# Grouping the triangular inverses of a chunked RWKV-7 kernel by four head pairs instead of two

## The chip, the cores and the metric

The kernel runs on one core of a Trainium2 chip. Its engines are TensorE (PE, with its weight loads PEld), VectorE (DVE), ScalarE (ACT), GpSimd (POOL) and SyncE (SP), whose queue issues most of the transfers. The metric is the device time of one execution in microseconds; the median of three runs of the kernel before is 1001.98 us (1001.26 to 1002.05).

## The reference

One layer of a hybrid block, for 512 tokens and 16 meta tokens of 2048 features, in float32. One input projection gives the streams of an RWKV-7 branch (r, k, v, a gate, and low-rank paths for the decay and for a) and of a gated short convolution (B, C, h, a gate). Both branches go through one output projection, a residual sum and an RMS norm. The RWKV-7 branch is a recurrence per head over a 64 x 64 state:

```python
def step(S, inp):
    r_t, w_t, k_t, v_t, kk_t, b_t = inp
    sa = jnp.einsum('bhvk,bhk->bhv', S, kk_t)
    S = (S * w_t[:, :, None, :]
         - sa[..., None] * b_t[:, :, None, :]
         + v_t[..., None] * k_t[:, :, None, :])
    y_t = jnp.einsum('bhvk,bhk->bhv', S, r_t)
    return S, y_t
```

There are 16 heads of 64. The kernel does not step through the tokens: it cuts them into 9 chunks (the meta tokens, padded to 64, and 8 of 64) and solves each chunk at once. For that it needs, per head and chunk, the inverse of a 64 x 64 unit triangular matrix made of the products of the keys with each other.

## The kernel before

**The stream.** The input projection is 65 tiles of 128 output features. Each tile is 16 steps of the contraction, each of three matmuls (the weights and the input are split in a high and a low part in a fast float32 format, and high x high, high x low and low x high are summed), over one or two ranges of tokens. `mains` (line 501) yields one matmul at a time, in the order of `plan` (line 127): keys, receptances and values of two head pairs, their gates, and a convolution tile set (C, h, B, gc) after each two pairs. Weights come in halves of a tile (`prefetch`, line 162) into three buffers; ACT casts each quarter (line 158) and DVE or POOL subtracts (line 159), into six buffers.

**The order of PE.** PE's order is written by hand; the order of the other engines is made by a planner that works by costs and priorities (`ahead()` raises the priority). All small work of the RWKV branch is put between matmuls of the stream: `fill(ns)` (line 572) issues stream matmuls worth `ns`, at 0.43 ns a column, and what is called behind it comes next on PE. `until` issues stream until a tile is done. The amounts are in `FW` (line 42). `later(ns, fn)` (line 553) puts off a transfer until the stream has gone on by `ns`, behind the latest weight load on SP's queue.

**A head pair.** `prepare(i)` (line 648), for each of the 8 pairs of heads: low-rank products (`low_rank`, four fills of 2200), scaled keys `bk` and receptances `ar`, then the Gram products (line 703: 32 matmuls and 4 for the meta chunk) which DVE masks into `gt` (line 729). `gt` has two buffers, `gt0` and `gt1`, one for each pair of a set of two. Its parts go out to DRAM: the key blocks to a scratch `sg` (line 786), from which 16 x 16 diagonal blocks come back as `d`; other parts to `opd`, the operands of the recurrence. DVE inverts the 16 x 16 blocks (lines 811 to 831), and `y` goes to the scratch `sx` (line 846), from which it comes back as the block diagonal start of the inverse, `xT` and a shifted copy `xo` (`load_inverse`, line 835). `sx` has two buffers that are cleared once (lines 310 to 314).

**The inverse.** `invert(two)` (line 873) takes two pairs. After a long fill (`solve` 24500 and `more`), two levels double the size of the inverted blocks, from 16 to 32 and from 32 to 64. Each level is: a transpose of `xT` on DVE, a cluster T of 64 matmuls with `gt` as the stationary operand (line 895; line 935 at the second level, 32 x 32), copies out of PSUM on ACT (lines 902, 943), a cluster Z of 64 matmuls (lines 909 and 911; 950 and 954), and DVE's merging of the result into `xT` (line 919 to 926; 960). Between the four clusters stand the fills `tr`, `lev`, `cp` + `tr`, `lev`. The clusters' results lie in the two PSUM banks `tz`. At last `put_inverse` stores `xT` to `opd`.

The calls are, in order, `prepare(0)`, `prepare(1)`, `invert` of both, and so on for 2 and 3, 4 and 5, 6 and 7 (line 1104). After the last one a fill of 19500 (`begin`) leads to `recur` (line 982), which goes through the 9 chunks with fills of 2900, 2900 and 5200 in between; then `split_mix` (line 1126) builds the operands of the output projection with fills in between, the rest of the stream is issued, and the output projection follows (`product`, line 1278; DVE splits its weights at line 1256).

Of the kernel before, what the change touches and what calls it, by code (L numbers as in the profile page):

```python
# [9 lines left out]
F32 = mybir.dt.float32  # L10
# [8 lines left out]
P = 128  # L19
# [24 lines left out]
    evac=34, start=1062, lora=2200, gram=8000, meta={0: 2000}, gram_b=13500, gram2=5500, misc=2000, v=2000, vt=1000, solve=24500, more={0: 5500, 2: 2400},  # L44
    tr=3200, lev=3000, cp=4200, out=1500, begin=19500, p=2900, u=2900, s=5200, last=3700, mix=2600,
)
# [52 lines left out]
def hymba_kernel(ctx: ExitStack, tc: tile.TileContext, xt, xtok, front, w_in, w_out, pv, lup, cst, msk, gf, out):  # L99
# [89 lines left out]

    scr_x = [dp.tile([SCR], F32, tag=f"sx{b}", name=f"sx{b}", bufs=1) for b in range(2)]  # L190

# [5 lines left out]
    def tm(name):  # L197
        return tp.tile([P, LP], F32, tag="tm", name=name, bufs=3)
# [110 lines left out]
    nc.sync.dma_start(ms, msk)  # L309
    zt = tm("zt")  # L310
    nc.gpsimd.memset(zt, 0.0)
    for b in range(2):
        for o, n in ((0, 293), (293, 292)):
            nc.sync.dma_start(scr_x[b][P * o : P * (o + n)].rearrange("(p f) -> p f", p=P), zt[:, 0:n])
    nc.gpsimd.memset(smask, 1.0)
# [324 lines left out]
    def behind(dst, src):  # L640
        with tc.issue_after(state["dma"]):
            nc.sync.dma_start(dst, src)


    def stash_later(ns, *a):
        later(ns, lambda: stash(*a))

    def prepare(i):
        p = i % 2
        until("k", i)  # L650
# [160 lines left out]
        for m in (2, 4, 8):  # L811
            for b in range(16 // (2 * m)):
# [18 lines left out]
                nc.vector.tensor_reduce(out=sub(y, o, o + m, [[16, m], [1, m]]), in_=pq, op=ALU.add, axis=AX.X)  # L831
        xT = cq.tile([P, NCH, CH], F32, tag=f"xT{p}", name=f"xT{i}")
        xo = cq.tile([P, 4, CH], F32, tag=f"xo{p}", name=f"xo{i}")

        def load_inverse():
            for h in range(2):
                nc.sync.dma_start(xT[64 * h : 64 * h + 64], rows(sx, h))
                nc.sync.dma_start(
                    xo[64 - 64 * h : 128 - 64 * h],
                    bass.AP(  # L840
                        tensor=sx.tensor, offset=sx.offset + (8 + 4 * h) * BLK,
                        ap=[[CH, CH], [16 * BLK, 4], [1, CH]],
                    ),
                )
# [25 lines left out]
        fill(FW["vt"])  # L870
        return dict(gt=gt, xT=xT, xo=xo, i=i)

    def invert(two):
        first = two[0]["i"]
        both = range(2)
        fill(FW["solve"] + FW["more"].get(first, 0))
        run_pending(float("inf"))


        def wide(name):  # L880
            return tr(name)[:, 0 : 8 * CH].rearrange("p (q k s) -> p q k s", q=2, s=CH)

        xn = [tr(f"xn{t['i']}") for t in two]
        with ahead():
            for q in both:
                state["turned"] = nc.vector.transpose(
                    xn[q][:, CH:LP], two[q]["xT"][:, 1:NCH].rearrange("p c s -> p (c s)")
                ).ins
        fill(FW["tr"])
        z = [pz.tile([P, 2, 4, CH], F32, tag="tz", name=f"t{first}_{e}") for e in range(2)]  # L890
        for q in both:
            for k in range(4):
                for e, c in ((0, 2 * k + 2), (1, 2 * k + 1)):
                    for h, hs, ho in heads:
                        nc.tensor.matmul(
                            z[e][ho if e else hs, q, k], two[q]["gt"][hs, h, c, 0:CH],
                            xn[q][hs, c * CH : (c + 1) * CH], start=True, stop=True,
                        )
        ts_ = [wide(f"ts{first}_{e}") for e in range(2)]
        with ahead():  # L900
            for e in range(2):
                nc.scalar.copy(ts_[e], z[e])
        fill(FW["lev"])
        z = [pz.tile([P, 2, 4, CH], F32, tag="tz", name=f"z{first}_{e}") for e in range(2)]
        for q in both:
            xT, xo = two[q]["xT"], two[q]["xo"]
            for k in range(4):
                for h, hs, ho in heads:
                    nc.tensor.matmul(z[0][hs, q, k], ts_[0][hs, q, k], xT[hs, 2 * k + 2], start=True, stop=True)
                for h, hs, ho in heads:  # L910
                    nc.tensor.matmul(z[1][hs, q, k], ts_[1][ho, q, k], xo[ho, k], start=True, stop=True)
        quads = [(h, slice(64 * h, 64 * h + 32), slice(64 * h + 32, 64 * h + 64)) for h in range(2)]
        other = [slice(96, 128), slice(32, 64)]
        xn = [tr(f"xm{t['i']}") for t in two]
        with ahead():
            for q in both:
                xT, xo = two[q]["xT"], two[q]["xo"]
                for e in range(2):
                    nc.vector.copy_predicated(
                        xT[:, 2 - e : NCH : 2], ms.unsqueeze(1).to_broadcast([P, 4, CH]), z[e][:, q]  # L920
                    )
                nc.vector.transpose(xn[q][:, CH:LP], xT[:, 1:NCH].rearrange("p c s -> p (c s)"))
            for q in both:
                xT, xo = two[q]["xT"], two[q]["xo"]
                for h, lo, hi in quads:
                    nc.vector.tensor_copy(xo[other[h], :, 32:CH], xT[hi, 1 : NCH - 1 : 2, 32:CH])
        fill(FW["cp"])

        fill(FW["tr"])
        z = [pz.tile([P, 2, 4, 32], F32, tag="tz", name=f"t2{first}_{e}") for e in range(2)]  # L930
        for q in both:
            for k in range(4):
                for e, c in ((0, 2 * k + 2), (1, 2 * k + 1)):
                    for h, lo, hi in quads:
                        nc.tensor.matmul(
                            z[e][other[h] if e else hi, q, k], two[q]["gt"][lo, h, c, 32:CH],
                            xn[q][lo, c * CH : c * CH + 32], start=True, stop=True,
                        )
        ts_ = [wide(f"tm{first}_{e}") for e in range(2)]
        with ahead():  # L940
            for e in range(2):
                for h, lo, hi in quads:
                    nc.scalar.copy(ts_[e][hi, :, :, 0:32], z[e][hi])
        fill(FW["lev"])
        z = [pz.tile([P, 2, 4, 32], F32, tag="tz", name=f"z2{first}_{e}") for e in range(2)]
        for q in both:
            xT, xo = two[q]["xT"], two[q]["xo"]
            for k in range(4):
                for h, lo, hi in quads:
                    nc.tensor.matmul(  # L950
                        z[0][lo, q, k], ts_[0][hi, q, k, 0:32], xT[hi, 2 * k + 2, 32:CH], start=True, stop=True
                    )
                for h, lo, hi in quads:
                    nc.tensor.matmul(
                        z[1][lo, q, k], ts_[1][other[h], q, k, 0:32], xo[other[h], k, 32:CH], start=True, stop=True
                    )
        for q in both:
            for e in range(2):
                for h, lo, hi in quads:
                    nc.vector.tensor_copy(two[q]["xT"][lo, 2 - e : NCH : 2, 32:CH], z[e][lo, q])  # L960

        def put_inverse():
            for t in two:
                if t["i"] % 2 == 0:
                    stash(t["i"], t["xT"], O_X, CH)
                else:
                    for h, hs, ho in heads:
                        stash(t["i"], t["xT"][hs], O_X, CH, 64 - 64 * h, 64)

        later(5500, put_inverse)  # L970
        fill(FW["out"] if first < NPAIR - 2 else FW["begin"])

# [130 lines left out]

    for i in range(0, NPAIR, 2):
        invert([prepare(i), prepare(i + 1)])
    until("g", NPAIR - 1)
# [461 lines left out]
```

## Time and profile before

| | |
|---|---|
| median of three runs | 1001.98 us |
| profiled execution | 1002.49 us, of it 1000.7 us span |
| PE busy | 989.0 us (99%) |
| DVE busy | 684.7 us (68%) |
| ACT busy | 395.3 us (39%) |
| POOL busy | 271.2 us (27%) |
| transfers | 174.82 MB; under 512 bytes 121568 of 185036 packets |
| PE's granted clock | 0.997 of full speed |

PE's matmuls are pipelined and the ends in the profile are modelled, so what PE spends is read from the starts. In a row of a timeline stand the start in us from the span's start, the length, the engine, the line of the kernel, the operation, what is written and read, the shapes and how many instructions the row merges; in brackets the idle time of the engine before the row and what ended it. In a row of groups stand the count, the busy time and the mean length.

### The profile page before, as it was taken

The numbers are of one execution on the slowest core, as the hardware profiler recorded it, in microseconds if no ns is written. First come the engines' busy times: TensorE is split into PE (matmuls) and PEld (weight loads), VectorE is DVE, ScalarE is ACT, GpSimd is POOL, SyncE is SP. The second block draws the span as 40 slices with busy tenths as digits, with TensorE's granted clock in tenths as the row PEclk, the third lists the DMA queues.
The fourth block names the chain that finished last, engine by engine and source line by source line (L and its number), as shares of the span: only waits on it lengthen the run. The fifth ranks groups of instructions, "written<-read, shape, count | busy, mean of one in ns | idle before, by whom it ended". The sixth has DMA issues, their size and how long they took to land.

```text
span 1000.7 us, 23699 instructions
## 1 busy us (share of the span) xinstructions
PE 989.0 (99%) x9723; PEld 912.3 (91%) x9723; DVE 684.7 (68%) x1247; ACT 395.3 (39%) x729; POOL 271.2 (27%) x292
## 2 busy tenths in 40 slices
PE   9999999999999999999999999999999999999996
PEld 7999999999998999998999998889888898888885
DVE  6777965588765679744669644244554697997897
ACT  7553423344313434322434322222222426546463
POOL 0122424234233424232324222223332333001001
PEclk9999999999999999999999999999999999999998
DMA  9425586555575273854374746877773688697654
GB/s 327 149 84 147 145 208 158 152 149 140 154 178 165 93 196 99 200 147 119 86 196 110 195 135 195 293 220 236 213 219 97 175 261 213 185 319 176 158 126 168
DMA packets 185036, 174.82 MB, mean 175 GB/s; under 512 B 121568, under 2 KB 142816, under 8 KB 184416
## 3 DMA queue, kind: packets, MB, share of 16 engines
q1 hardware_dynamic: 182336, 164.40, 56.9%
q0 software_dynamic: 2304, 8.39, 4.8%
q8 instruction: 76, 1.25, 0.5%
q10 hardware_dynamic: 288, 0.52, 0.1%
q14 instruction: 32, 0.26, 0.1%
HBM read 136.92 MB, written 36.35 MB: 173 GB/s over the span
## 4 chain that ended last, share of the span: by engine, by line
PE 90%; DVE 5%; DMA 2%; issue 1%; SPq 0%; ACT 0%; POOL 0%; DVEq 0%; ACTq 0%; POOLq 0%
PE ps_v L346 9%; PE ps_k L346 9%; PE ps_h L346 9%; PE ps_g L346 9%; PE ps_r L346 9%; PE ps_B L346 9%; PE ps_gc L346 9%; PE ps_C L346 8%; PE M L1285 5%; PE P L1285 2%; DVE o L1256 2%; PE g L703 2%; PE Q L1285 1%; PE ps_lora L346 1%; PE zs L1048 1%
## 5 line engine op out<-in xcount | busy, mean ns | idle before, releaser
L158 ACT CAST w<-wr 128x512 fp32r<-128x512 f32 x252 | 153.4, 620 | 286.5 <-PE ps_C L346 48.2
L159 POOL TENSOR_TENSOR w<-wr,w 128x512 fp32r<-128x512 f32 x119 | 170.7, 1436 | 343.7 <-ACT w L158 290.9
L159 DVE TENSOR_TENSOR w<-wr,w 128x512 fp32r<-128x512 f32 x133 | 98.1, 743 | 114.4 <-ACT w L158 114.1
L346 PE MATMUL ps_k<-xh,w 128*128 128x272 f32 (+1 forms) x512 | 95.3, 284 | 0.0
L346 PE MATMUL ps_v<-xh,w 128*128 128x256 f32 (+1 forms) x512 | 95.3, 284 | 0.0
L346 PE MATMUL ps_r<-xh,w 128*128 128x258 f32 (+1 forms) x512 | 94.9, 281 | 0.0
L346 PE MATMUL ps_h<-xh,w 128*128 128x256 f32 (+1 forms) x512 | 94.0, 282 | 0.0
L346 PE MATMUL ps_C<-xh,w 128*128 128x256 f32 (+1 forms) x512 | 93.1, 281 | 0.0
L346 PE MATMUL ps_g<-xh,w 128*128 128x256 f32 (+1 forms) x512 | 91.5, 280 | 0.0
L346 PE MATMUL ps_B<-xh,w 128*128 128x512 f32 x256 | 83.8, 395 | 0.0
L346 PE MATMUL ps_gc<-xh,w 128*128 128x512 f32 x256 | 81.3, 392 | 0.0
L346 PEld LDWEIGHTS ps_k<-xh,w 128*128 128x128 f32 x512 | 80.0, 188 | 0.4
L346 PEld LDWEIGHTS ps_v<-xh,w 128*128 128x128 f32 x512 | 80.0, 188 | 0.3
L346 PEld LDWEIGHTS ps_r<-xh,w 128*128 128x128 f32 x512 | 79.9, 188 | 0.1
L346 PEld LDWEIGHTS ps_h<-xh,w 128*128 128x128 f32 x512 | 79.3, 188 | 0.7
L346 PEld LDWEIGHTS ps_C<-xh,w 128*128 128x128 f32 x512 | 79.2, 188 | 0.6
L346 PEld LDWEIGHTS ps_g<-xh,w 128*128 128x128 f32 x512 | 78.7, 188 | 0.2
L346 PE MATMUL ps_h<-xl,w 128*128 128x258 f32 (+1 forms) x256 | 71.9, 281 | 1.0 <-issue 1.0
L346 PE MATMUL ps_k<-xl,w 128*128 128x272 f32 (+1 forms) x256 | 72.6, 284 | 0.0
L346 PE MATMUL ps_v<-xl,w 128*128 128x272 f32 (+1 forms) x256 | 72.5, 283 | 0.0
L346 PE MATMUL ps_r<-xl,w 128*128 128x258 f32 (+1 forms) x256 | 72.2, 282 | 0.0
L346 PE MATMUL ps_g<-xl,w 128*128 128x258 f32 (+1 forms) x256 | 72.0, 281 | 0.0
(337 smaller groups left out, 2264.1 us busy)
## 6 DMA issues: line engine op xcount, KB each, us to landing
wr<-in_w_in_dram SPq DMA_DIRECT2D x126, 512.0 KB
ct<-opd SPq DMA_DIRECT2D x64, 288.0 KB
wo<-in_w_out_dram SPq DMA_DIRECT2D x24, 512.0 KB
x<-in_w_out_dram POOLq DMA_DIRECT2D x16, 512.0 KB, 6.4
opd<-ar SPq DMA_DIRECT2D x8, 576.0 KB
opd<-gt SPq DMA_DIRECT2D x16, 288.0 KB
opd<-bt SPq DMA_DIRECT2D x64, 64.0 KB
x<-in_w_out_dram SPq DMA_DIRECT2D x8, 512.0 KB
```

What stands on the lines that cost most here:

```text
L158: nc.scalar.copy(hi, rq)
L159: low[q] = eng.tensor_tensor(out=lo, in0=rq, in1=hi.bitcast(F32), op=ALU.subtract).ins
L346: nc.tensor.matmul(ps[r], ww[:, w], xx[:, kt, a:b], start=(kt == 0 and n == 0), stop=(kt == KT - 1 and n == 2))
L703: nc.tensor.matmul(z[h][:, c - c0], bk[hs, c, h : h + 2, :].rearrange("p a s -> p (a s)"), ar[hs, c].rearrange("p a s -> p (a s)"), start= ...
L1048: nc.tensor.matmul(d[hs, j], w, x[hs], start=(a == 0), stop=(a == b - 1))
L1256: last = nc.vector.tensor_tensor(out=lo, in0=rq, in1=hi.bitcast(F32), op=ALU.subtract)
L1285: nc.tensor.matmul(bank[s], left(prod, jj, m, s), w, start=(jj == 0 and n == 0), stop=(jj == 7 and n == 2))
```

## The change

The pairs are taken four at a time. `prepare` runs for four pairs, and one `invert` then takes all four, so that each of its clusters has 128 matmuls (T and Z at both levels) and there are two calls instead of four.

- Where the first inverse of each four was (after pairs 1 and 5), `wait_only` issues the same fills without clusters.
- `invert(first)` has a fill of 3000 more (`quad`) ahead of it, 4300 instead of 3000 (`lev4`) between T and Z and between T2 and Z2, and 10000 (`cp4`) instead of 4200 and 3200 between Z and T2. Its results take four PSUM banks: `tz` twice, `misc` and `ser`.
- `gt` has one buffer (`gt0`) for all pairs. The key blocks of four pairs come back from `sg` (now four buffers) into `gk`, which lies where `gt1` was: two loads of 64 partitions x 9 blocks x 64 values per pair, put off by 17000 and 18500.
- `xT` and `xo` of the first two of four pairs lie in buffers of their own, those of the third and fourth in the buffer `bk` of the scaled keys, from the time when the fourth pair no longer needs these. Their loads come at 21000 (third) and 22500 (fourth).
- `sx` has four buffers; the second two are cleared after pair 1.
- `put_inverse` is put off by 5500, 6000, 6500 and 7000 for the four pairs. The special times for pair 1 (22500 and 24500) are gone: 20500 and 22500 as for the other odd pairs.

```diff
-    tr=3200, lev=3000, cp=4200, out=1500, begin=19500, p=2900, ...
+    tr=3200, lev=3000, lev4=4300, cp4=10000, quad=3000, cp=4200, out=1500, begin=19500, p=2900, ...
...
-        gt = cq.tile([P, 2, NCH, P], F32, tag=f"gt{p}", name=f"gt{i}")
+        gt = cq.tile([P, 2, NCH, P], F32, tag="gt0", name=f"gt{i}")
...
-        sg = dp.tile([SCR], F32, tag="sg", name=f"sg{i}")
+        sg = dp.tile([SCR], F32, tag="sg", name=f"sg{i}", bufs=4)
...
-        sx = scr_x[i % 2]
+        sx = scr_x[q4]
...
+        if q4 == 0:
+            gk = cq.tile([P, 2, NCH, P], F32, tag="gt1", name=f"gk{i}").rearrange("p a c s -> p (a c s)")
+            blocks_of["all"] = gk.rearrange("p (q c s) -> p q c s", q=4, s=CH)
+        gk = blocks_of["all"]
+
+        def load_blocks(h):
+            nc.sync.dma_start(gk[64 * h : 64 * h + 64, q4], rows(sg, h))
+
+        for h in range(2):
+            later(17000 + 1500 * h, lambda h=h: load_blocks(h))
...
+        if q4 < 2:
+            xT = cq.tile([P, NCH, CH], F32, tag=f"xT{q4}", name=f"xT{i}")
+            xo = cq.tile([P, 4, CH], F32, tag=f"xo{q4}", name=f"xo{i}")
+            inverse_of[i] = xT, xo
+        elif q4 == 3:
+            t = cq.tile([P, NCH, 3, CH], F32, tag="bk", name=f"xx{i}").rearrange("p a b c -> p (a b c)")
...
-        later((22500 if i == 1 else 20500) if p else 29000, lambda: nc.sync.dma_start(blocks(sx), y))
-        later((24500 if i == 1 else 22500) if p else 33000, load_inverse)
+        later(20500 if p else 29000, lambda: nc.sync.dma_start(blocks(sx), y))
+        if q4 == 3:
+            later(21000, lambda: load_inverse(i - 1))
+        if q4 != 2:
+            later(22500 if p else 33000, lambda: load_inverse(i))
...
+    def wait_only(first):
+        fill(sum(FW[n] for n in ("solve", "tr", "lev", "cp", "tr", "lev", "out")) + FW["more"].get(first, 0))
...
-    def invert(two):
+    def invert(first):
+        gk, quad = blocks_of["all"], range(4)
+        xs = [inverse_of[first + q] for q in quad]
+        fill(FW["solve"] + FW["quad"])
...
-        z = [pz.tile([P, 2, 4, CH], F32, tag="tz", name=f"t{first}_{e}") for e in range(2)]
-        for q in both:
+        z, zt = products(CH, "t")
+        for q in quad:
             for k in range(4):
                 for e, c in ((0, 2 * k + 2), (1, 2 * k + 1)):
                     for h, hs, ho in heads:
                         nc.tensor.matmul(
-                            z[e][ho if e else hs, q, k], two[q]["gt"][hs, h, c, 0:CH],
+                            z[q][e][ho if e else hs, k], gk[hs, q, c],
                             xn[q][hs, c * CH : (c + 1) * CH], start=True, stop=True,
                         )
...
-        fill(FW["lev"])
+        fill(FW["lev4"])
...
-        fill(FW["cp"])
-
-        fill(FW["tr"])
+        fill(FW["cp4"])
...
-    for i in range(0, NPAIR, 2):
-        invert([prepare(i), prepare(i + 1)])
+    for first in (0, 4):
+        for i in range(first, first + 4):
+            prepare(i)
+            if i == 1:
+                clear_scratch((2, 3))
+            if i == first + 1:
+                wait_only(first)
+        invert(first)
```

More of the change, by code (lines that the diff above doesn't have):

```diff
@@ L903, in invert @@
-        fill(FW["lev"])
-        z = [pz.tile([P, 2, 4, CH], F32, tag="tz", name=f"z{first}_{e}") for e in range(2)]
-        for q in both:
-            xT, xo = two[q]["xT"], two[q]["xo"]
+            for d, p in zip(tt_, zt):
+                nc.scalar.copy(d, p)
+        fill(FW["lev4"])
+        z, zt = products(CH, "z")
+        for q in quad:
+            xT, xo = xs[q]
             for k in range(4):
                 for h, hs, ho in heads:
-                    nc.tensor.matmul(z[0][hs, q, k], ts_[0][hs, q, k], xT[hs, 2 * k + 2], start=True, stop=True)
+                    nc.tensor.matmul(z[q][0][hs, k], ts_[q][0][hs, k], xT[hs, 2 * k + 2], start=True, stop=True)
@@ L910, in invert @@
                 for h, hs, ho in heads:
-                    nc.tensor.matmul(z[1][hs, q, k], ts_[1][ho, q, k], xo[ho, k], start=True, stop=True)
+                    nc.tensor.matmul(z[q][1][hs, k], ts_[q][1][ho, k], xo[ho, k], start=True, stop=True)
         quads = [(h, slice(64 * h, 64 * h + 32), slice(64 * h + 32, 64 * h + 64)) for h in range(2)]
         other = [slice(96, 128), slice(32, 64)]
-        xn = [tr(f"xm{t['i']}") for t in two]
+        xn = [tr(f"xm{first + q}") for q in quad]
@@ L925, in invert @@
                 for h, lo, hi in quads:
                     nc.vector.tensor_copy(xo[other[h], :, 32:CH], xT[hi, 1 : NCH - 1 : 2, 32:CH])
-        fill(FW["cp"])
-        fill(FW["tr"])
-        z = [pz.tile([P, 2, 4, 32], F32, tag="tz", name=f"t2{first}_{e}") for e in range(2)]
-        for q in both:
+        fill(FW["cp4"])
+        z, zt = products(32, "t2")
+        for q in quad:
             for k in range(4):
@@ L935, in invert @@
                         nc.tensor.matmul(
-                            z[e][other[h] if e else hi, q, k], two[q]["gt"][lo, h, c, 32:CH],
+                            z[q][e][other[h] if e else hi, k], gk[lo, q, c, 32:CH],
                             xn[q][lo, c * CH : c * CH + 32], start=True, stop=True,
                         )
-        ts_ = [wide(f"tm{first}_{e}") for e in range(2)]
+        ts_, tt_ = wide("tm")
         with ahead():
-            for e in range(2):
+            for d, p in zip(tt_, zt):
                 for h, lo, hi in quads:
[L943 to L947, printed above, removed]
+                    nc.scalar.copy(d[hi, :, :, 0:32], p[hi])
+        fill(FW["lev4"])
+        z, zt = products(32, "z2")
+        for q in quad:
+            xT, xo = xs[q]
             for k in range(4):
```

93 lines of the change are left out of this document (53 added, 40 removed).

## The prediction

> **What bounds the kernel now.** I read the page first, then who TensorE (PE) waited for, then PE's timeline around two clusters of the inverse and one of the recurrence, then VectorE (DVE), ScalarE (ACT) and the SP queue where the changed work runs, and last the busy time of DVE by stretch at the end.
>
> ```profile
> span 1000.7 us, 23699 instructions
> PE 989.0 (99%) x9723; PEld 912.3 (91%) x9723; DVE 684.7 (68%) x1247; ACT 395.3 (39%) x729; POOL 271.2 (27%) x292
> PE ps_h L346 <- issue: 1.0, 1, 1.0
> PE M L1285 <- DVE o L1256: 0.5, 1, 0.5
> 142.16 11.20 PE ps_h L346 x96
> ```
>
> PE is busy for 989.0 of 1000.7 us and its list of waits holds hardly more than these two. PE's order is written by hand: one stream of projection matmuls, with the small matmuls of the inverse put in between after a stated amount of stream. So the time is the sum of what PE issues, and two things can move it: PE work that goes, and a PE wait that comes. A tile of the stream that the planner prices at 514 columns x 48 x 0.43 ns = 10.6 us takes 11.20 (last row): planner times below become real ones times 1.056.
>
> **What a cluster costs beyond its matmuls.** A busy PE is not a full one, so I take starts, not lengths.
>
> ```profile
> 170.50 0.41 PE L346 MATMUL ps_k<-xh,w 128*128 128x272 f32 x2
> 170.84 1.16 PE L895 MATMUL t<-xn,gt 64*64 64x64 f32 x64
> 171.94 0.40 PE L346 MATMUL ps_k<-xl,w 128*128 128x272 f32 x1
> 172.17 0.42 PE L346 MATMUL ps_k<-xh,w 128*128 128x272 f32 x2
> 172.43 0.28 PE L346 MATMUL ps_k<-xl,w 128*128 128x272 f32 x1
> ...
> 184.44 0.28 PE L346 MATMUL ps_r<-xh,w 128*128 128x258 f32 x1
> 184.65 0.75 PE L935 MATMUL t<-xm,gt 32*32 32x32 f32 x64
> 185.33 0.39 PE L346 MATMUL ps_r<-xh,w 128*128 128x258 f32 x1
> 185.55 0.28 PE L346 MATMUL ps_r<-xl,w 128*128 128x258 f32 x1
> ...
> 767.81 0.28 PE L346 MATMUL ps_h<-xh,w 128*128 128x256 f32 x1
> 768.02 0.69 PE L1013 MATMUL rz<-pn,ct 64*64 64x64 f32 x32
> 768.64 0.38 PE L346 MATMUL ps_h<-xh,w 128*128 128x256 f32 x1
> 768.87 0.29 PE L346 MATMUL ps_h<-xl,w 128*128 128x256 f32 x1
> 768.99 0.39 PE L346 MATMUL ps_h<-xh,w 128*128 128x256 f32 x2
> ...
> L935 PE MATMUL t<-xm,gt x256: 191/191/212, 184.6 to 602.4; 32*32 32x32 f32 x128
> ```
>
> A stream matmul starts every 0.13 us (172.17 to 172.43 is two), or 0.12 at 256 columns (768.87 to 768.99). Without the cluster the stream would have gone on at 170.75; it is back in step at 172.17, which is one place after 172.04. So 64 matmuls of 64x64 cost 1.29 us. The cluster of 32 in the recurrence costs (768.87 - 0.12) - (767.81 + 0.12) = 0.82. The difference, 0.47 for 32 matmuls, is 14.7 ns each, so 0.35 us of each cluster is a fixed price of going in and out. For the 32x32 kind: (185.55 - 0.12) - (184.44 + 0.12) = 0.87 us; one matmul lasts 191 ns (last row), so 64 of them start within 0.75 - 0.19 = 0.56, and 0.30 is fixed.
>
> **The change part by part.**
>
> *Fewer clusters.* Four pairs instead of two go into each of the four clusters (T, Z, T2, Z2): 16 clusters of 64 matmuls become 8 of 128. Matmuls, shapes and their order within a pair stay. Gone are four fixed prices of each kind: 4 x 0.35 + 4 x 0.30 = **2.6 us**, all on PE, which sets the end. The lower bound of this gain is nothing (rival 3), the upper one 2.6 plus the waits quoted above.
>
> *Filler.* The first inverse of each half is replaced by the same amount of stream without clusters, so pairs 2 and 6 start where they did. The merged inverse needs 24500 + 3000 + 3200 + 4300 + 10000 + 4300 = 49300 ns of stream up to Z2, before it was 41100. In the first half this is absorbed: pair 4 waits for its keys anyway (planner time 278.6, and it is there at 273.5). In the second half the recurrence, and all that follows it, sits 8.2 x 1.056 = 8.7 us later in the stream. By the fills in the code 694 planner us of stream are there in all, and the last mixed tile is placed at 674, after the change at 682.5: PE does not run out of filler; it is DVE that pays, below.
>
> *Chains between clusters.* They double.
>
> ```profile
> 172.04 1.08 ACT L902 COPY ts<-t 128x512 f32<-128x512 f32 x2 [3.78 <-PE t L895]
> 185.44 1.52 ACT L943 COPY tm<-t 32x256 f32<-32x256 f32 x4 [0.73 <-PE t L935]
> ...
> 174.90 0.69 DVE L159 TENSOR_TENSOR w<-wr,w 128x512 fp32r<-128x512 f32 x1 [3.12 <-ACT w L158]
> 176.60 1.11 DVE L919 COPY_PREDICATED xT<-ms,z 128x256 f32<-128x256 int32 x3 [1.01 <-PE z L911]
> 179.67 1.39 DVE L926 COPY xo<-xT 32x128 f32<-32x128 f32 x3
> 183.49 0.69 DVE L159 TENSOR_TENSOR w<-wr,w 128x512 fp32r<-128x512 f32 x1
> ```
>
> ts: 2 x 1.08 = 2.2 us under 4300 of fill; tm: 2 x 1.52 = 3.0 under 4300; predicated copies, transposes and xo copies: 176.60 to 181.06 is 4.5 us for two pairs, 9 for four, under 10000. Cost nothing; if the fill is not there, PE waits one for one. The later Z2 copies come after the cluster and hold only the banks of the next pair's low-rank products: pairs 0 and 1 are copied first and own both banks that these need, as before.
>
> *Key blocks.* Sixteen loads of 64 x 9 pieces of 256 bytes, twice per pair, 17.0 and 18.5 us after the pair's stores; four more zero fills; four scratch buffers.
>
> ```profile
> 291.77 0.64 SPq L838 DMA_DIRECT2D xo<-sx  x1
> q1 hardware_dynamic: 182336, 164.40, 56.9%
> ```
>
> The nearest issue costs 0.64 us of SP, so 16 x 0.64 = 10 us of SP over the span, behind stores that are long done. A packet takes 0.569 x 16 x 1000.7 / 182336 = 50 ns of one DMA engine, so a load of 576 takes 1.8 us of all sixteen. Both lie beside PE: nothing, unless weights come late (rival 2).
>
> *One Gram buffer.* The next pair's Gram products now wait for the four stores of the pair before: last one due 8.5 planner us after its store point, the next Gram comes 26 or more after it. Nothing; the cover is over 15 us. POOL clears 48 columns of this buffer ahead of them, and a clear that is queued early would hold POOL's weight splits for that long.
>
> *The scaled keys' buffer.* Pair 4 writes its scaled keys where the inverses of 2 and 3 lie, whose stores are due at planner 278.4 and 278.9; the keys are scaled after the fourth low-rank fill at 288.6. Some 9 us of cover; without it PE waits at pair 4's Gram. Inverse loads of pair 2 stand ahead of those of pair 3 on SP: 4 x 0.6 us more, ahead of the weights queued behind. Pair 1's are earlier by 2 us with nobody waiting.
>
> *The end.* After the recurrence DVE builds the eight mixed tiles.
>
> ```profile
> 795.22 1.66 DVE L1141 SCALAR_TENSOR_TENSOR mix<-mix,hl,rb 128x512 f32<-128x512 f32 x1
> 796.80 0.68 DVE L401 SCALAR_TENSOR_TENSOR gc<-th_c,gc 128x512 f32<-128x512 f32 x1
> 798.07 0.68 DVE L468 SCALAR_TENSOR_TENSOR mix<-cv,gc 128x512 f32<-128x512 f32 x1
> 798.67 0.68 DVE L159 TENSOR_TENSOR w<-wr,w 128x512 fp32r<-128x512 f32 x1
> ...
> 804.00:828.90 24.90, 24.90 (x164) 22.80 (x163) 24.25 (x35) 9.64 (x19) 8.92 (x5) 1.00 0.87 262
> 828.90:838.40 9.50, 9.50 (x43) 7.87 (x42) 4.91 (x6) 1.87 (x3) 4.76 (x4) 1.00 0.88 234
> 838.40:846.40 8.00, 8.00 (x36) 6.58 (x36) 6.90 (x9) 6.09 (x9) 0.87 (x1) 1.00 1.02 254
> 846.40:875.10 28.70, 28.19 (x123) 22.63 (x121) 28.70 (x38) 16.89 (x29) 2.63 (x3) 1.00 0.64 167
> ```
>
> Columns: stretch, its length, then busy time of PE, PEld, DVE, ACT, POOL. The output product begins at 838.4. From 795 to 829 DVE is full, then it has 9.50 - 4.91 = 4.6 and 8.00 - 6.90 = 1.1 us free, and from 846.4 it is full for 28.70 of 28.70 us while PE loses 0.5 to it. The change puts the mixed tiles 8.7 us later against the stream. They no longer meet the three stream instructions of 796.80 to 798.67 (2.0), and the full stretch has 24.90 - 24.25 = 0.65 free. What is left over, 8.7 - 2.0 - 0.65 - 5.7 = **0.4 us**, PE would wait near 847. Bounds: 0 if the splits that PE needs go first, 3.0 if only the 5.7 are used (8.7 - 5.7). I take 0.4, since all three rows lie in the stretch itself.
>
> **Sum.** The profiled execution took 1002.49 us (span 1000.7 and 1.8 around it): 1002.49 - 2.6 + 0.4 = 1000.3. It lies 0.5 above the median of the runs, 1001.98; so 999.8 for the median.
>
> **The rivals.**
>
> *1, DVE's lateness at the end eats the gain.* The mixed tiles are paced by their loads as well, so the free time before 838 may not be used. Then PE waits 3.0: 1001.98 - 2.6 + 3.0 = 1002.4, no change. For it: DVE has no room from 846.4 on, so what is late there stays late. Against: the 5.7 us free before.
>
> *2, slower: the doubled DVE burst makes weights late.*
>
> ```profile
> 293.09 0.73 ACT L446 ACTIVATE cv<-u,pvt 128x512 f32<-128x512 f32 x1 [10.96 <-POOL u L444]
> 293.72 2.17 ACT L158 CAST w<-wr 128x512 fp32r<-128x512 f32 x4
> 295.31 3.48 DVE L159 TENSOR_TENSOR w<-wr,w 128x512 fp32r<-128x512 f32 x2
> 298.71 0.70 DVE L886 STREAM_TRANSPOSE xn<-xT 128x512 f32<-128x512 f32 x1
> ```
>
> Just ahead of the place of the first merged inverse, four weight casts stand behind an instruction that ACT waited 10.96 us for, so the weights for the tile in hand are split only while it runs. The burst of 4.5 us that keeps weight splits off DVE (174.90 to 183.49 above) becomes 9. If the weights have nothing in hand there, PE waits the 4.5 that are added: 999.8 + 4.5 = 1004.3; at both merged inverses 1008.8. It decides for slower from a burst that is 2.2 us over the lead of the weights. Against: no PE wait is listed there now, POOL splits half of the weights, and the second inverse has no such stretch. The Trainium skill, page TensorEngine Tiling (Array Packing), section Performance Considerations, holds that packing speeds up TensorE but not the emptying of PSUM, which may become the bottleneck; by that rule this rival is the case and the time 1004.3. The rows of ACT and DVE above show the emptying covered at two pairs, and none shows four.
>
> *3, the change doesn't do what it says: the fixed price goes with each 64 matmuls, not with the cluster.* Then only the 0.4 is left: 1002.4. Against: 32 and 64 matmuls differ by 0.47 us, well under half of 1.29.
>
> **Chances.** A difference of 0.2%, 2.0 us, is about what a measurement of this kernel can tell from no change. Forecast 999.8 (faster): 0.45. Rival 1, no change: 0.20. Rival 2, slower: 0.30. Rival 3, no change: 0.05. So faster 0.45, same 0.25, slower 0.30. The forecast's own range is 998.6 (no loss at the end, some of the quoted waits gone) to 1000.4. To leave out no more than 0.2, the whole range goes up past rival 1 and past one late burst, short of two: 998.6 to 1006.
>
> **What would show it.** Eight clusters of 128 with 2.24 and 1.44 us between the stream's steps show the saving right; a wider gap shows rival 3. PE's list of waits should stay as short, with DVE's splits of the output weights near 845 as its longest entry. Waits of PE for weight splits at 290 to 325 us or near 590 show rival 2; a wait at a Gram cluster would show that a shared buffer was not free, and a wait at T that the key blocks came late. Any of these of over 3 us makes the forecast wrong.

## The result, and the profile after

The changed kernel takes 1015.5 us (median of 4 runs, 1014.34 to 1016.66), the kernel before 1001.97 in the same session: ratio 1.0137, 95% interval 1.0125 to 1.0149. It is 1.4% slower, above the whole range of the prediction. The profiled execution took 1014.34 us.

The first lines of the page of the changed kernel:

```profile
span 1012.6 us, 23741 instructions
...
PE 990.9 (98%) x9723; PEld 914.4 (90%) x9723; DVE 684.5 (68%) x1247; ACT 392.8 (39%) x729; POOL 276.8 (27%) x293
```

And its list of PE's waits (who waited, for whom, us in total, how often, the longest):

```profile
PE M L1333 <- ACT o L1303: 6.4, 1, 6.4
PE zy L1094 <- issue: 2.0, 2, 1.8
PE ps_r L350 <- ACT w L158: 1.9, 1, 1.9
...
PE ps_gc L350 <- DVE w L159: 0.9, 1, 0.9
PE ps_r L350 <- DVE w L159: 0.5, 1, 0.5
```

DVE does the same amount of work as before (684.5 against 684.7 us) and no engine has become the bound. What is new is a handful of PE waits in four places: r2 (the receptance tile of pair 2) near 177 us, gc2 (the third gate tile of the convolution) near 456 us, the recurrence, and M (the first product of the output projection) at 857 us. `zy`, and `rz` further below, are products of the recurrence. None lies at an inverse.

PE's timeline at two of the merged clusters shows what the change was to bring:

```profile
299.63 0.39 PE L350 MATMUL ps_B<-xh,w 128*128 128x512 f32 x1
299.95 2.10 PE L938 MATMUL t<-xn,gk 64*64 64x64 f32 x128
301.97 0.50 PE L350 MATMUL ps_B<-xh,w 128*128 128x512 f32 x1
...
319.32 0.28 PE L350 MATMUL ps_k<-xl,w 128*128 128x256 f32 x1
319.52 1.46 PE L976 MATMUL t<-xm,gk 32*32 32x32 f32 x128
320.91 0.50 PE L350 MATMUL ps_k<-xh,w 128*128 128x256 f32 x2
```

There are 2.34 us between the stream's steps at the first (in a 512-column tile, whose own step is 0.1 us longer than that of the tile for which 2.24 was forecast), and 1.59 us at the second. From the starts around all clusters, less the steps that the stream itself would have taken, the 16 of before cost 17.4 us and the 8 of after 15.3: the saving is there, 2.1 us.

The loss is larger than the listed waits, since PE's clock is halved at two of them: right behind the waits at r2, and at M from 854.7 us on, while PE still waits there. Two stretches of the windows view (stretch, length, busy time and count of PE, PEld, DVE, ACT, POOL, granted clock, DMA share, GB/s):

```profile
178.90:182.20 3.30, 3.30 (x18) 3.30 (x17) 2.61 (x2) 0.81 (x2) 3.30 (x3) 0.50 0.55 154
...
855.00:861.40 6.40, 3.88 (x9) 2.77 (x9) 3.90 (x6) 4.55 (x8) 0.89 (x1) 0.50 0.79 239
```

At a clock of 0.50 the 512-column matmuls of M start every 427 ns instead of 227. From the starts in the trace, the profiled execution loses at r2 2.7 us of waits and 1.7 of half clock; 1.1 at gc2 (456 us); 1.0 more than before in the recurrence; at M 6.0 more and 2.1 of half clock. Less the 2.1 saved, that is 12.5 us; the spans differ by 11.9, and 0.5 of the rest is the start, where this execution was ahead (PE's fourth run of stream matmuls begins at 9.46 us instead of 9.92).

### The wait at r2

ACT's timeline, after the change:

```profile
165.13 1.13 ACT L158 CAST w<-wr 128x512 fp32r<-128x512 f32 x2
175.86 0.73 ACT L384 ACTIVATE sh_k<-pr_k,pvt 128x528 f32<-128x528 f32 x1 [9.60 <-DVE pr_k L377]
176.50 3.21 ACT L158 CAST w<-wr 128x512 fp32r<-128x512 f32 x6
```

and before it:

```profile
165.56 2.70 ACT L158 CAST w<-wr 128x512 fp32r<-128x512 f32 x5
...
174.25 0.62 ACT L158 CAST w<-wr 128x512 fp32r<-128x512 f32 x1 [0.61 <-PE ps_k L346]
...
181.90 0.74 ACT L380 ACTIVATE sh_k<-pr_k,pvt 128x528 f32<-128x528 f32 x1 [2.79 <-DVE pr_k L373]
```

ACT was idle for 9.60 us. `sh_k` of pair 2 reads the end of the stream's tile k2 (the keys of that pair), and six casts of weights stand behind it, among them those for r2, which follows k2 on PE. In the kernel before, these casts stand ahead of it. The order of ACT's queue is made when the program is built, and ACT kept to it: by the trace's semaphores the load for the first of the six casts had landed at 172.1 us, and the cast started at 176.50, behind `sh_k`. SP's queue shows that the weight loads which feed the casts are late too. After:

```profile
159.58 0.40 SPq L166 DMA_DIRECT2D wr<-in_w_in_dram  x1
...
165.02 0.58 SPq L864 DMA_DIRECT2D xT<-sx  x1
...
167.75 0.54 SPq L166 DMA_DIRECT2D wr<-in_w_in_dram  x1
```

Before, the same two loads:

```profile
151.09 0.38 SPq L166 DMA_DIRECT2D wr<-in_w_in_dram  x1
...
158.73 0.35 SPq L166 DMA_DIRECT2D wr<-in_w_in_dram  x1
```

They come 8.5 and 9.0 us later. Between them now stand the store and the loads of pair 1's inverse (line 864); two key-block loads and, further up, four zero fills stand ahead of both.

### The wait at the output projection

Four queues of the changed kernel, one fence each (SP, DVE, ACT, POOL):

```profile
848.71 0.33 SPq L1281 DMA_DIRECT2D x<-in_w_out_dram  x1
```

```profile
847.99 0.69 DVE L472 SCALAR_TENSOR_TENSOR mix<-cv,gc 128x512 f32<-128x512 f32 x1
```

```profile
856.85 1.66 ACT L1303 CAST o<-x 128x512 fp32r<-128x512 f32 x3 [4.67 <-DMA x<-in_w_out_dram]
```

```profile
840.71 4.62 POOL L464 TENSOR_TENSOR cv<-cv,b 128x512 f32<-128x512 f32 x1 [9.34 <-DVE b L377]
845.28 2.96 POOL L1290 DMA_DIRECT2D x<-in_w_out_dram  x3
```

X3, the first load of the fourth column block of the output weights, is issued only when DVE has read the last gate tile gc7 (line 472), and it lands 8 us after that; its cast starts at 856.85, and PE has waited 6.4 us for it. In the kernel before the same load stands at

```profile
831.78 0.33 SPq L1233 DMA_DIRECT2D x<-in_w_out_dram  x1
```

X3 lies where the buffers of the stream's small tiles were (b7 and gc7 among them, from the last B and gc tiles of the stream). In the built program the three buffers of the ring `tm` begin at bytes 119296, 121600 and 123904 of a partition and X3 takes 124608 to 128704, so it lies on the third. Before the change the last tile in the third buffer is b7; after it, gc7, and the load is issued 17 us later (848.71 against 831.78). The zero tile of `clear_scratch((2, 3))` is one more tile of that ring, and it has turned it.

### The profile page after: what moved, and what is told of

Read it like the earlier page. It is cut to its first block, busy times and chain, and to the rows that moved or that the text cites. A ratio compares the mean times of both kernels' runs of the same rounds, so it can differ in the third digit from the quotient of the medians.

```text
span 1012.6 us, 23741 instructions
## 1 busy us (share of the span) xinstructions
PE 990.9 (98%) x9723; PEld 914.4 (90%) x9723; DVE 684.5 (68%) x1247; ACT 392.8 (39%) x729; POOL 276.8 (27%) x293
## 4 chain that ended last, share of the span: by engine, by line
PE 92%; DVE 3%; DMA 3%; issue 1%; ACT 1%; SPq 0%; DVEq 0%; POOL 0%; ACTq 0%
PE ps_v L350 9%; PE ps_k L350 9%; PE ps_r L350 9%; PE ps_g L350 9%; PE ps_C L350 8%; PE ps_h L350 8%; PE ps_B L350 8%; PE ps_gc L350 8%; PE M L1333 7%; PE P L1333 4%; PE Q L1333 2%; PE g L709 2%; DVE mix L1189 1%; DMA x<-in_w_out_dram 1%; PE ps_lora L350 1%; PE zs L1090 1%
## 5 line engine op out<-in xcount | busy, mean ns | idle before, releaser
L159 DVE TENSOR_TENSOR w<-wr,w 128x512 fp32r<-128x512 f32 x133 | 103.6, 784 | 104.5 <-ACT w L158 104.3
```

The costliest lines, as they stand in the source:

```text
L159: low[q] = eng.tensor_tensor(out=lo, in0=rq, in1=hi.bitcast(F32), op=ALU.subtract).ins
```

## The experiments

**First question: the ring, or the lateness?** Theory A: the extra zero tile put X3 on gc7's buffer. Theory B: recurrence and mixed tiles stand 8.7 us later in the stream.

*e1, clear all at the start.*

```diff
-    clear_scratch((0, 1))
+    clear_scratch((0, 1, 2, 3))
...
-            if i == 1:
-                clear_scratch((2, 3))
```

> All four scratch buffers are cleared at the start from one zero tile, so that no zero tile is allocated after pair 1 and no zero fill stands on SP's queue at 144 us; all else as in the changed kernel. Theory A (the extra zero tile turns the rotation of the three tm buffers by one, and X3 lands on the buffer of the last gate tile gc7): the load of X3 is issued some 17 us earlier, the 6.4 us wait of PE at the product M and the half clock behind it go, about -8 us: 1007.5 us; if the four zero fills also make the weights of r2 late at 177 us, up to 4.4 us more: 1003. Theory B (the tail waits because the recurrence and the mixed tiles run 8.7 us later in the stream): the wait at M stays, 1015.5 us, or 1011 if only r2's wait goes.

Measured: 1011.35 us, 1.0096 (1.0081 to 1.0111). X3 is off gc7's buffer, and the wait of 6.4 with its half clock is gone, but not all waits at M are:

```profile
PE M L1331 <- DVE o L1302: 1.4, 2, 1.0
PE M L1331 <- ACT o L1301: 0.9, 1, 0.9
...
PE M L1331 <- DVE w L159: 0.5, 1, 0.5
```

The waits at r2 are the same 1.9 and 0.5 us, so the zero fills on SP's queue don't make them. Without them the load for the first of the six casts lands at 170.2 us, 1.9 earlier, and the cast still starts behind `sh_k`, at 177.13: it is the order on ACT that holds it. The half clock behind the waits at r2 was twice as long in this execution, which costs 1.7 us more:

```profile
178.30:184.90 6.60, 6.08 (x28) 6.09 (x29) 4.10 (x4) 2.65 (x5) 4.94 (x3) 0.50 0.48 138
```

So M gained 5.7 us (6.4 to 2.8, and the 2.1), and r2 took 1.7 back: 4.0, measured 4.2.

*e2, the kernel before with one more tile of the ring.*

```diff
         invert([prepare(i), prepare(i + 1)])
+        if i == 0:
+            nc.gpsimd.memset(tm("one")[:, 0:1], 0.0)
```

> The kernel before with one more tile of the tm ring, taken after the first inverse and touched by a memset of one column; nothing else. Theory A: the wait at the product M that the changed kernel shows appears here too, PE waits some 6 us for the cast of X3 at M1 and runs at half clock after it: about 1010 us. Theory B: nothing happens, 1002.0 us.

Measured: 1002.94 us, 1.0011 (1.0002 to 1.0021). X3 does lie on gc7's buffer and its load moves behind gc7, from 831.78 to 841.27, yet PE waits little:

```profile
PE M L1287 <- ACT o L1257: 0.9, 1, 0.9
PE M L1287 <- DVE o L1258: 0.6, 2, 0.4
```

Theory A as stated falls: the ring alone costs 1.0 us.

*e3, two more tiles of the ring in the changed kernel.*

```diff
         invert(first)
+        if first == 0:
+            for n in ("one", "two"):
+                nc.gpsimd.memset(tm(n)[:, 0:1], 0.0)
```

> The changed kernel with two more tiles of the tm ring after the first inverse, so that the ring stands at the end as in the kernel before (one zero tile and two more are three). The zero fills and all of SP's load near 144 to 178 us stay. Theory A: the wait at M goes and the wait at r2 near 177 us stays: about 1007.5 us. Theory B: both stay, 1015.5 us.

Measured: 1015.53 us, 1.0132 (1.0110 to 1.0154); the wait at M is 6.6. The edit did not do what it was to do: in the built program both new tiles got the same buffer (119296), since the first was free again when the second was asked for, and gc7 stayed in the third. It tells nothing for or against either theory.

*e4, the recurrence back at its old place.*

```diff
-    ... begin=19500, ...
+    ... begin=11300, ...
```

> The changed kernel with the filling between the second inverse and the recurrence cut from 19500 to 11300, so that the recurrence and all that follows it stand in the stream where they stood before the change; the ring of tm tiles is that of the changed kernel. Theory A: X3 still waits for gc7, the wait at M stays, 1015 us (within 1.5). Theory B: the wait at M goes, about 1007 us.

Measured: 1015.79 us, 1.0141 (1.0124 to 1.0157). The total is as A expected and the reason is not. The waits at M are 0.8 and 0.7 with X3 still on gc7, as in e2; the time is lost at the start of the recurrence instead, again with half clock (from 636 us, 6.8 long):

```profile
PE rz L1038 <- DMA ct<-opd: 4.3, 8, 1.8
```

The recurrence reads its operands back from DRAM, and these can't be loaded before the merged inverse has ended and stored. So the 8.2 us of filler ahead of it were in use.

Neither cause does it alone. The new theory is that they do more together than in sum: X3's load waits for gc7, and with the late recurrence DVE reads gc7 later and the load itself is slower (from issue to cast 8.1 us in the changed kernel, 5.5 in e2). In e2 DVE reads gc7 13.2 us after PE began that tile, in the changed kernel 16.1 (starts in the traces: 840.55 - 827.3, 847.99 - 831.9). And of the transfers that add weights on POOL's queue, e2 has

```profile
831.41 1.07 POOL L1244 DMA_DIRECT2D x<-in_w_out_dram  x1
835.09 0.88 POOL L1244 DMA_DIRECT2D x<-in_w_out_dram  x1 [2.61 <-DVE w L159]
840.06 0.86 POOL L1244 DMA_DIRECT2D x<-in_w_out_dram  x1 [4.09 <-DVE w L159]
```

ahead of X3's load at 841.27; in the changed kernel the same three stand on POOL's queue behind the product `cv` (line 464) and start together at 845.28 to 848, right ahead of X3 at 848.71. That product waits for DVE to read b7, which it does 8.3 us after PE's last matmul of that tile (839.95 against 831.68) where it was 1.5 in e2 (828.51 against 827.05), and it takes 4.62 us where it took 1.74.

**The same two causes in the kernel before.** *e10* is the kernel before with only the lateness, *e11* with both.

```diff
-    ... begin=19500, ...
+    ... begin=27700, ...
```

> The kernel before with the filling between its last inverse and the recurrence raised from 19500 to 27700, so that the recurrence and all behind it stand 8.2 us of stream later, where the change put them; no merged cluster, X3 on b7's buffer as before. Two-cause theory: lateness alone costs waits at M of 2 to 3 us in all (as in the changed kernel with the scratch cleared at the start): 1004.5 us. My prediction's price for it was 0.4 us: 1002.4.

> The kernel before with both: 27700 instead of 19500, and one more tile of the tm ring after the first inverse, so that X3 lies on gc7's buffer. Two-cause theory: the changed kernel's loss at the output projection appears here whole, without any merged inverse: a wait of some 6 us at M for the cast of X3 and half clock behind it, 1002 + 8.5 = 1010.5 us. If the causes only add (1.0 us for the ring, 2.5 for the lateness): 1005.5 us. If the loss needs something else of the change: 1003 us.

Measured: e10 1007.07 us, 1.0050 (1.0034 to 1.0065); e11 1012.09 us, 1.0109 (1.0094 to 1.0124). Waits of e10:

```profile
PE zy L1052 <- issue: 2.2, 2, 1.5
PE M L1285 <- DVE o L1256: 1.5, 2, 1.0
...
PE M L1285 <- DVE w L159: 1.3, 1, 1.3
PE M L1285 <- ACT o L1255: 1.0, 1, 1.0
```

and of e11:

```profile
PE M L1287 <- ACT o L1257: 5.9, 1, 5.9
```

| kernel | X3 lies on | recurrence | waits at M, us | against before, us |
|---|---|---|---|---|
| before | b7 | early | 0.5 | |
| e2 | gc7 | early | 1.5 | +1.0 |
| e10 | b7 | late | 3.8 | +5.1 |
| e11 | gc7 | late | 6.4, with half clock | +10.1 |

Together they cost 10.1, not 1.0 + 5.1: the difference is X3's load coming behind everything (8.3 us from issue to cast), and the half clock, which here lies almost whole on matmuls (some 3 us). The changed kernel's loss at M is there whole without a merged cluster. e10 cost twice what I expected of it: the recurrence itself loses 1.2 us more (2.2 against 1.0), and M 3.3 more. X3's load is late there even on b7's buffer (issued at 840.39, in the kernel before at 831.78), since DVE reads b7 at 837.41 instead of 828.81.

**Second question: what makes r2 late?** Theory C: the order on ACT's queue. Theory D: the added loads on SP's queue, by their time.

*e5, key blocks of pairs 0 and 1 loaded past the place.*

```diff
-            later(17000 + 1500 * h, lambda h=h: load_blocks(h))
+            later((70000 if i < 2 else 17000) + 1500 * h, lambda h=h: load_blocks(h))
```

> The changed kernel with the key-block loads of pairs 0 and 1 put off to 70000 ns of stream behind their place, past r2's tile; nothing else. In the program ACT still has two casts of r2's and k2's weights ahead of the key activation sh_k of pair 2, as in the changed kernel. Theory C (PE's wait at r2 near 177 us comes from that order on ACT's queue): the wait of 1.9 and 0.5 us stays, 1015.5 us within 1. Theory D (it comes from the time that the two loads take on SP's queue ahead of the weight load of 159.6 us): the wait is gone or halved, 1011 to 1013.5 us.

Measured: 1014.94 us, 1.0139 (1.0123 to 1.0155), and waits of 1.9 and 0.5 at r2 as in the changed kernel. With e1, which moved the zero fills, theory D falls for all the added transfers.

*e6, pair 1's inverse at its old times.*

```diff
-        later(20500 if p else 29000, lambda: nc.sync.dma_start(blocks(sx), y))
+        later((22500 if i == 1 else 20500) if p else 29000, lambda: nc.sync.dma_start(blocks(sx), y))
...
-            later(22500 if p else 33000, lambda: load_inverse(i))
+            later((24500 if i == 1 else 22500) if p else 33000, lambda: load_inverse(i))
```

> The changed kernel with the store and the loads of pair 1's inverse back at 22500 and 24500 ns of stream, where the kernel before has them; nothing else. In the program four casts, not two, now stand ahead of sh_k of pair 2 on ACT's queue (five or more in the kernel before). Theory C (the order on ACT's queue): PE's wait at r2 goes, and the half clock behind it: 1015.5 - 4.4 = 1011 us. Theory D (the key-block loads and zero fills on SP's queue): the wait stays, 1015.5 us.

Measured: 1011.27 us, 1.0094 (1.0080 to 1.0108): 4.2 us less than the changed kernel, where 4.4 was expected, and no wait at r2 is listed. Its ACT has four casts ahead of `sh_k`:

```profile
165.54 1.12 ACT L158 CAST w<-wr 128x512 fp32r<-128x512 f32 x2
168.71 1.14 ACT L158 CAST w<-wr 128x512 fp32r<-128x512 f32 x2 [2.04 <-DMA wr<-in_w_in_dram]
176.21 0.74 ACT L384 ACTIVATE sh_k<-pr_k,pvt 128x528 f32<-128x528 f32 x1 [6.36 <-DVE pr_k L377]
```

ACT still stands for 6.36 us, and it costs nothing, since what PE needs next is ahead. On SP's queue of e6 the weight load stands ahead of the inverse that in the changed kernel, at 167.75, stands behind it:

```profile
163.18 1.90 SPq L166 DMA_DIRECT2D wr<-in_w_in_dram  x1
166.78 0.58 SPq L864 DMA_DIRECT2D xT<-sx  x1
```

Moving one store and four loads by 2 us of stream changed SP's order around a weight load, and with it the planner's order on ACT. e6 changes both orders at once; that the one on ACT holds PE follows from the load that had landed 4 us before its cast in the changed kernel, and from e1.

**Third question: is the account whole, and does it lead to a better kernel?**

*e8, shorter fillings inside the inverse*, so that the recurrence can start earlier:

```diff
-    ... lev4=4300, cp4=10000, ...
+    ... lev4=3000, cp4=6500, ...
```

> The changed kernel with the fillings inside the inverse cut: lev4 from 4300 to 3000 (twice) and cp4 from 10000 to 6500, so that both inverses end 6.1 us of stream earlier and the recurrence starts about 6 us earlier; the three tm buffers stand as in the changed kernel. If the tail's loss is the product of two causes (X3 on gc7's buffer, and the mixed tiles some 3 us late on DVE), the wait of 6.4 us at M falls to about 1.5 as in the run with the early recurrence, and the half clock goes: 1015.5 - 7 = 1008.5 us. If the position of the recurrence has no part in it: 1015.5 us. If the shorter fillings are too short for the chains on ACT and DVE, PE waits at Z or T2: each such wait is under 2 us, twice.

Measured: 1017.44 us, 1.0153 (1.0137 to 1.0168), slower still. No PE wait is listed at Z, T2 or Z2, so the chains are covered at the shorter fillings. But the recurrence now comes before its operands (waits of 2.1 us at `rz`, and half clock), and the wait at M is 4.2 with half clock, where 1.5 was expected. DVE reads gc7 here as early as in e2, 13.3 us after PE began that tile (850.28 against 837.0), and yet X3's load takes 8.8 us (issued at 851.00, cast at 859.80), with the three adding transfers at 846.2 to 850.6 right ahead of it. So the slow landing alone makes this wait: 0.9 us as in e2, and 3.3 more of landing (8.8 against 5.5). In e2 and e4, where only one of the three is issued in the 5 us ahead of it, the load takes at most 5.5 us; that the three make it slow fits all these runs, but no run moved them alone.

*e9, four edits:* those of e1, e5, e6 and e8 together.

> The changed kernel with four things at once: all scratch buffers cleared at the start (X3 off gc7's buffer), the key blocks of pairs 0 and 1 loaded later, pair 1's inverse at its old times, and the shorter fillings of lev4 and cp4. If the account of the losses is whole (r2 4.4 us, the tail about 8.8, the recurrence about 1), what is left is the saving of the merged clusters less small waits: 1015.5 - 14 = 1001 us, down to 999.4 if the tail stands as in the kernel before. If something else of the change costs time that has not been seen, it stays at 1004 or above.

Measured: 1007.17 us, 1.0051 (1.0038 to 1.0063). The waits at r2 are gone and M waits 0.5, as in the kernel before; of what is left, most is

```profile
PE rz L1038 <- DMA ct<-opd: 2.1, 5, 0.5
```

which I had not put into the expected sum. The clock goes down at 632.4 us, behind the first four of these five short waits:

```profile
633.50:640.00 6.50, 6.50 (x59) 6.35 (x59) 0.00 (x0) 1.01 (x2) 0.70 (x1) 0.56 0.92 345
```

*e12*, the loads of the first chunk raised ahead of two weight loads on SP's queue:

```diff
-        load_chunk(ch, 0, range(NPAIR), ops)
+        with ahead():
+            load_chunk(ch, 0, range(NPAIR), ops)
```

> The changed kernel with the four edits of the run before (scratch cleared at the start, key blocks of pairs 0 and 1 later, pair 1's inverse at its old times, shorter fillings in the inverse) and the loads of the recurrence's first chunk raised in priority, so that on SP's queue they stand ahead of two weight loads, not behind them. The 2.1 us of waits for these loads at 630 us and the half clock behind them (together some 5 us) go: 1007.2 - 5 = 1002 us, the time of the kernel before; below it by up to 1.5 us if the small waits of the recurrence and at gc2 stay as they were. If the two weight loads that now come later make the stream wait: 1004 us or more.

Measured: 1002.28 us, 1.0001 (0.9992 to 1.0010): 4.9 us less than e9, as expected, and no wait at `rz`. Left are a wait of 1.3 in the recurrence, some of under half a microsecond, and one of 0.9 at gc2. At gc2 ACT shows the picture of r2 again:

```profile
442.85 0.72 ACT L450 ACTIVATE cv<-u,pvt 128x512 f32<-128x512 f32 x1 [11.83 <-POOL u L448]
443.48 2.69 ACT L158 CAST w<-wr 128x512 fp32r<-128x512 f32 x5
```

*e13*, three weight loads raised on SP's queue, so that their casts are ordered ahead of this `cv`:

```diff
-            state["dma"] = nc.sync.dma_start(raw, stream[j]).ins
+            with tc.high_priority(offset=8000 if j in (70, 71, 72) else 0):
+                state["dma"] = nc.sync.dma_start(raw, stream[j]).ins
```

> The run before with three weight loads (numbers 70 to 72 of the stream) raised in priority on SP's queue; in the program four casts more then stand ahead of the convolution's cv2 on ACT's queue, as in the kernel before the change, and not behind it. If PE's wait of 0.9 us at gc2 near 454 us is the same thing as the wait at r2 (casts queued behind an operation that waits for the end of a tile of the stream), it goes: 1002.3 - 1.1 = 1001.2 us. If it comes from something else, it stays: 1002.3 us.

Measured: 1000.62 us, 0.9986 (0.9977 to 0.9995) of the kernel before; of e12's ratio, 1.0001, that is 1.5 us less. All of PE's waits (`pwarm` is the kernel's start, the same in every run):

```profile
PE pwarm L208 <- DVE cold L205: 1.4, 1, 1.4
PE zy L1096 <- issue: 0.6, 1, 0.6
PE M L1333 <- DVE o L1304: 0.5, 1, 0.5
```

This is the merged inverse with its side effects taken away, and it is faster than both kernels: than the one before by 1.2 us in the medians (1.4 by the ratio) of the 2.1 that the clusters save. Where the rest went I did not find; half of the interval's width is 0.9 us. The kernel before has no wait at `rz` or gc2 that these edits could take away; its fillings were not shortened in any run.

## Why the prediction was wrong

- **Fewer clusters, 2.6 us.** Right in kind, 2.1 in size. The 64x64 clusters saved 1.4 as worked out (4 x 0.35). The 32x32 ones saved 0.7 instead of 1.2: in clusters of 128 their matmuls start every 9.8 to 10.6 ns, where 8.9 to 9.3 was measured in those of 64. Rival 3 is out.
- **Filler, chains between clusters, one Gram buffer, the scaled keys' buffer, key blocks.** Right as far as PE's waits tell: PE waits at no T, Z, T2, Z2 or Gram cluster, e8 shows room for still shorter fillings, and e5 shows that the key-block loads near r2 cost nothing that can be measured.
- **"Pair 1's are earlier by 2 us with nobody waiting."** This step failed, with 4.2 us (e6). I asked who waits for the moved loads. The question was who is queued behind them: a weight load on SP, and through the planner the order of casts on ACT. The wait at gc2, 1.1 us, is of the same kind (e13) and had no term either. I had the sign of it in hand, since I quoted the same picture near 293 us (four casts behind a `cv` that ACT waits 10.96 us for).
- **"Four more zero fills": nothing.** As transfers that is right (e1). What I did not count was the tile they come from: one more allocation in a ring of three, which put the first load of another phase, 700 us later, behind another tile.
- **"The end", 0.4 us, bounds 0 to 3.0.** This step failed most. The lateness alone costs 3.3 us at M, just above my upper bound, and 1.2 in the recurrence, for which I had no term (e10, 5.1 in all); with the ring it is 8.1 at M in the changed kernel. I added DVE's free time over a stretch as if late work could flow into it; but the mixed tiles' work and the reading of the stream's tiles are in one queue, b7 is read 6.8 us later against PE than in e2 and gc7 2.9, and three transfers behind b7's product on POOL then come right ahead of X3's load.
- **Rival 1** named the right place, and its price was near what the lateness alone cost there (3.0 against 3.3 in e10); it had neither the recurrence nor the ring. **Rival 2** had the right sign and almost the right kind, weights late for the stream, but at r2 and by the order of a queue; at its own places, 290 to 325 us and 590, the stream lost nothing against the kernel before. By the rule of the Trainium skill named there (TensorEngine Tiling (Array Packing), Performance Considerations), the copies out of PSUM may become the bottleneck; in this case's trace they have not for four pairs, as PE waits for none of them.
- **The range** priced one such loss. Two causes that each cost 1 to 5 us came to 10 together, and the waits at r2 and M brought half clock with them, which no term of the sum had.

## What to carry to other kernels

When a change moves a transfer or adds a tile, ask what is queued behind it on that queue, and what the builder will now order or place differently: an operation that waits for the end of a tile in PE's stream must not get ahead of the casts for the next one, and a ring that turns by one tile changes what a later phase waits for. A shift of work against PE's stream is not paid from the free time of an engine over a stretch, but at the one load or split that now comes last; test it by shifting that work alone in the kernel before, which here gave the loss without the change. Waits of a PE that is otherwise full are to be counted with the half clock that can come with them once they add up to some 2 us within 3.4 (here 1.6 was enough at one place and 1.9 not at another): 1.7 to 3.4 us more, where PE is busy again while it lasts.

## What the hardware showed that I had not expected

- **Half clock after short waits.** Waits of 1.9 and 0.5 us within 3 us (r2) or four of about 0.4, 1.7 in all, within 3 us (e9) were enough. Yet a single wait of 2.0 us in e4 (near 770 us) and one of 1.8 in the changed kernel (736) passed without it. By the trace's clock records a stretch at half clock is 3.413 or 6.827 us long, and the same waits at r2 gave the first in the changed kernel and the second in e1; why, no run shows. The stretches of one execution begin whole numbers of 3.413 us apart (178.86 and 854.70 in the changed kernel are 198.0 of these, 179.53 and 636.92 in e8 134.0). If time is cut into such lengths from there, the two waits that passed are each cut by a border (0.8 and 1.2 us, 0.5 and 1.3), and idle time of 1.6 us inside one length (r2 in e8) or more brought half clock, of 1.58 (M in e1) or less did not, but for one case: at M in e11 1.9 us did not, so the idle time is not all that counts. The Trainium skill, page TensorE: Matmul & The Clock Gate, section What's actually happening, speaks of a window of 3413 ns that runs freely and is not reset; the lengths and the starts agree with it. It has the clock halved after an idle window; at r2 and in e9 PE was idle for less than one, and that was enough.
- **Small matmuls packed in the array** start every 14.8 to 15.0 ns (64x64) and every 8.9 to 10.6 ns (32x32), and the longer cluster of the 32x32 kind was the slower one per matmul. Why, no run shows.
- **A load's place in the queue cost more than its length.** The four inverse loads take 2.5 us of SP (0.58 to 0.65 each); two microseconds of stream in their place were worth 4.2 us.
